# A hybrid decoder layer: both feed-forward products by seven products of quarters, with sums added in DRAM

## The chip, the core and the metric

The kernel runs on one core of a Trainium2 chip. The time is the device time of one execution, in microseconds; the lower it is, the better. TensorE (PE) has a clock that the chip grants at one of two levels, 1.2 and 2.4 GHz; the profile shows 2.4 GHz as a granted clock of 1.00 and 1.2 GHz as 0.50.

## The reference

One layer on a sequence of 512 tokens, 2048 wide, with 8192 hidden columns, all in float32:

```
h = rms_norm(x)
p = h @ w_in                      # three kinds of heads: gating MLP, short conv, dilated attention
x = x + concat(A, B, C) @ w_out
h = rms_norm(x, mlp_norm)
x = x + square(relu(h @ w_mlp_in)) @ w_mlp_out
```

The change concerns the last two lines: a product of 512 x 2048 by 2048 x 8192, which the text calls the first product (FF1), and one of 512 x 8192 by 8192 x 2048, the second product (FF2).

## The kernel before

**Three matmuls for a product.** Every float32 operand is split into a high part and a low part. ScalarE (ACT) rounds to the high part (a cast), VectorE (DVE) subtracts it to get the low part, and a product is then high by high, high by low, and low by high, summed in PSUM (`mm3`, L162 to L164). Activations lie transposed, with features on the 128 partitions and the 512 tokens along the free dimension. A weight tile is the stationary operand and a matmul is 512 or 256 tokens wide. `wh` and `wl` are the parts of weights, three buffers each; `xhl` holds the parts of the normalised activations (later of hidden tiles), `pt` is a PSUM tile.

**Plain groups.** A group of 512 output columns (`tr_group`) has eight pieces of weights, of two K-tiles (128 rows of the contraction) each: the piece is loaded (`wr`, in the pool's tag "raw", three buffers), cast, its low part subtracted, and then multiplied, 4 column tiles x 3 matmuls for each K-tile. Weights are prepared two pieces ahead (AHEAD = 2, `stream`).

**Groups of seven products.** Twenty-nine groups of FF1, of 256 columns each, are done with the scheme of Strassen and Winograd: the operands are cut into quarters, seven products of quarters take the place of eight, and each one needs sums of quarters. The class `Strassen` loads four quarters of the weights (`wq`, L821), forms sums of them (`ws` and in place, L826 to L832), splits each of the seven operands, multiplies (`product`, L845 and L846), and combines the results in an output tile `c` (six parts of 256 columns) with `p` as room for products 0 and 3 (L849, L862). A step of a product is a pair of matmuls: one of 512 (high weights by high and low activations side by side) and one of 256 (low weights by high activations), and DVE adds the two halves afterwards. The activations' sums (`tt`, four operands with high and low parts) are made once, by tasks, in FF1's first plain group (`x_sums`, L784, from the float32 activations `xg` in the pool "x1"). That pool is closed before the first quarter is loaded, and the pool "quarters" is opened in its place. `c` has a single buffer there. It is stored to `hd` in DRAM (L877).

**Order.** `tasks` is a list of small pieces of work: after each K-tile of a plain group, and after each product of a seven-product group, `step` runs the next one, so that this work stands between weights on DVE and ACT; `flush` runs all that are left. In FF1 a scheduler sets the order. From FF1's last group on, DVE and ACT work in the order of the program (`ordr`); matmuls and DMAs are still ordered by the scheduler. A hidden tile is read back from `hd` by GpSimd's (POOL's) queue (L899), squared with relu, multiplied by the reciprocal mean square `rbc` (L903, L904) and split, by `hid_tasks`.

**FF1 and FF2.** FF1 is one plain group of 512 columns, 29 seven-product groups, one plain group of 256. FF2 goes through the hidden columns in four chunks of 2048, and in each through four plain groups of 512 output columns. The sums over chunks stay in SBUF: `acc`, 16 tiles, starts as the residual `x1d` (L939) and each group's PSUM is added to it (L950). Two buffers (`hid` and `xhl`) hold the hidden tiles of alternate chunks. The last group's last pieces are ordered by output tile, with the final tile in two halves of 256.

## Time and profile before

| | before |
|---|---|
| time, median of three runs | 2067.32 us (2066.99 to 2067.97) |
| time of the profiled execution | 2066.59 us |
| its span in the profile | 2064.9 us |
| TensorE busy | 2051.5 us, 99% |
| VectorE busy | 1198.2 us, 58% |
| ScalarE busy | 677.5 us, 33% |
| GpSimd busy | 100.6 us, 5% |
| mean granted clock | 0.999 |

The span is the time between the first and the last instruction that the profiler recorded on the core; the rest of the execution's time lies around it. Busy shares are means over the whole span. The rest of the profile is read by stages: the time of each engine in a stretch, the price of one instruction of a given shape, and, at a hole in an engine's work, what ended it (written behind the instruction as the idle time and its releaser). Matmuls overlap, so the price of one is the distance between starts, not its own duration; the same is true of DVE to a small degree.

### The profile page before, as it was taken

The numbers are of one execution on the slowest core, as the hardware profiler recorded it, in microseconds if no ns is written. First come the engines' busy times: TensorE is split into PE (matmuls) and PEld (weight loads), VectorE is DVE, ScalarE is ACT, GpSimd is POOL, SyncE is SP. The second block draws the span as 40 slices with busy tenths as digits, with TensorE's granted clock in tenths as the row PEclk, the third lists the DMA queues.
The fourth block names the chain that finished last, engine by engine and source line by source line (L and its number), as shares of the span: only waits on it lengthen the run. The fifth ranks groups of instructions, "written<-read, shape, count | busy, mean of one in ns | idle before, by whom it ended". The sixth has DMA issues, their size and how long they took to land.

```text
span 2064.9 us, 25736 instructions
## 1 busy us (share of the span) xinstructions
PE 2051.5 (99%) x10274; PEld 1751.2 (85%) x10274; DVE 1198.2 (58%) x1675; ACT 677.5 (33%) x905; POOL 100.6 (5%) x194
## 2 busy tenths in 40 slices
PE   9999999999999999999999999989999999999999
PEld 9999888888888888888888888878888888888888
DVE  5443453534334489899998998866624632652222
ACT  5334442322233443344334333333312321322121
POOL 0000000100000000000000000120100000000000
PEclk9999999999999999999999999999999999999999
DMA  7423222433533454444444344364433432432332
GB/s 248 133 75 108 72 72 69 125 99 97 193 113 123 130 148 141 145 122 141 132 126 148 121 141 128 103 241 156 143 101 108 147 114 100 136 124 95 119 116 82
DMA packets 247016, 259.69 MB, mean 126 GB/s; under 512 B 11748, under 2 KB 179940, under 8 KB 246896
## 3 DMA queue, kind: packets, MB, share of 16 engines
q1 hardware_dynamic: 229888, 206.08, 32.3%
q0 software_dynamic: 14560, 47.75, 6.7%
q10 hardware_dynamic: 2448, 4.23, 0.6%
q8 instruction: 80, 1.31, 0.3%
q14 instruction: 40, 0.33, 0.1%
HBM read 232.81 MB, written 25.19 MB: 125 GB/s over the span
## 4 chain that ended last, share of the span: by engine, by line
PE 71%; issue 26%; POOL 2%; DMA 0%; DVE 0%; ACT 0%; POOLq 0%; DVEq 0%; ACTq 0%
PE pt L162 18%; PE pt L163 18%; PE pt L164 18%; PE pn L162 5%; PE pn L163 5%; PE pn L164 5%; POOL hd L877 1%; PE pt L845 1%; PE pt L846 1%; PE sc L529 0%; PE et L542 0%; PE qt L463 0%; ACT wh L262 0%; DMA acc<-x1d 0%; PE warm L124 0%
## 5 line engine op out<-in xcount | busy, mean ns | idle before, releaser
L263 DVE TENSOR_TENSOR wl<-wr,wh 128x1024 fp32r<-128x1024 f32 (+2 forms) x287 | 321.4, 1121 | 612.3 <-ACT wh L262 574.8
L262 ACT CAST wh<-wr 128x1024 fp32r<-128x1024 f32 (+2 forms) x287 | 277.5, 968 | 710.7 <-PE pt L163 578.7
L162 PE MATMUL pt<-xhl,wh 128*128 128x512 f32 (+1 forms) x912 | 352.6, 387 | 0.0
L163 PE MATMUL pt<-xhl,wh 128*128 128x512 f32 (+1 forms) x912 | 351.6, 386 | 0.0
L164 PE MATMUL pt<-xhl,wl 128*128 128x512 f32 (+1 forms) x912 | 351.5, 385 | 0.0
L845 PE MATMUL pt<-tt,wh 128*128 128x512 f32 x928 | 330.5, 399 | 0.0
L846 PE MATMUL pt<-tt,wl 128*128 128x256 f32 x928 | 260.6, 281 | 0.0
L845 PE MATMUL pt<-xhl,wh 128*128 128x512 f32 x696 | 248.5, 399 | 0.0
L262 ACT CAST wh<-wq 128x1024 fp32r<-128x1024 f32 x145 | 152.3, 1050 | 246.2 <-PE pt L845 233.8
L845 PEld LDWEIGHTS pt<-tt,wh 128*128 128x128 f32 x928 | 174.4, 188 | 43.6
L162 PE MATMUL pt<-hid,wh 128*128 128x512 f32 x512 | 200.4, 391 | 6.9 <-ACT wh L262 6.9
L263 DVE TENSOR_TENSOR wl<-wq,wh 128x1024 fp32r<-128x1024 f32 x145 | 177.1, 1222 | 43.5 <-ACT wh L262 40.9
L162 PEld LDWEIGHTS pt<-xhl,wh 128*128 128x128 f32 x912 | 171.3, 188 | 34.6 <-issue 0.2
L164 PEld LDWEIGHTS pt<-xhl,wl 128*128 128x128 f32 x912 | 171.3, 188 | 34.6
L163 PEld LDWEIGHTS pt<-xhl,wh 128*128 128x128 f32 x912 | 171.3, 188 | 34.2 <-issue 0.2
L163 PE MATMUL pt<-hid,wh 128*128 128x512 f32 x512 | 199.9, 391 | 0.0
L164 PE MATMUL pt<-hid,wl 128*128 128x512 f32 x512 | 198.2, 390 | 0.1
L846 PE MATMUL pt<-xhl,wl 128*128 128x256 f32 x696 | 195.5, 281 | 0.0
L162 PE MATMUL pn<-wh,xhl 128*128 128x384 f32 (+2 forms) x512 | 185.8, 366 | 1.3 <-DVE qn L440 1.3
L163 PE MATMUL pn<-wl,xhl 128*128 128x384 f32 (+2 forms) x512 | 179.4, 350 | 0.0
L164 PE MATMUL pn<-wh,xhl 128*128 128x384 f32 (+2 forms) x512 | 179.3, 350 | 0.0
L846 PEld LDWEIGHTS pt<-tt,wl 128*128 128x128 f32 x928 | 175.3, 189 | 0.0
(203 smaller groups left out, 2571.9 us busy)
## 6 DMA issues: line engine op xcount, KB each, us to landing
wr<-in_w_mlp_out_dram SPq DMA_DIRECT2D x128, 512.0 KB, 3.5
wq<-in_w_mlp_in_dram SPq DMA_DIRECT2D x116, 512.0 KB, 4.1
wr<-in_w_in_dram SPq DMA_DIRECT2D x144, 128.0 KB, 2.4
wr<-in_w_out_dram SPq DMA_DIRECT2D x32, 512.0 KB, 3.5
hd<-c POOLq DMA_DIRECT2D x58, 256.0 KB, 2.6
hs<-hd POOLq DMA_DIRECT2D x56, 256.0 KB, 2.9
wr<-in_w_in_dram SPq DMA_DIRECT2D x24, 512.0 KB, 3.5
wr<-in_w_in_dram SPq DMA_DIRECT2D x31, 384.0 KB, 3.5
```

Source lines behind the costliest of these rows:

```text
L162: nc.tensor.matmul(ps, lhsT=ah, rhs=bh, start=start, stop=False)
L163: nc.tensor.matmul(ps, lhsT=ah, rhs=bl, start=False, stop=False)
L164: last[0] = nc.tensor.matmul(ps, lhsT=al, rhs=bh, start=False, stop=stop)
L262: ordr(nc.scalar.copy(out=dst_h, in_=src))
L263: ordr(nc.vector.tensor_tensor(out=dst_l, in0=src, in1=dst_h.bitcast(F32), op=ALU.subtract))
L845: nc.tensor.matmul(pv, lhsT=h[:, m], rhs=b, start=m == 0, stop=False)
L846: nc.tensor.matmul(pv[:, 1], lhsT=l[:, m], rhs=b[:, 0], start=False, stop=m == KT // 2 - 1)
L877: nc.gpsimd.dma_start(out=hd[self.c0 // P + n], in_=c[:, 2 + 2 * n:4 + 2 * n].rearrange("p h t -> p (h t)"))
```

## The change

- **FF1.** The first plain group has 256 columns in place of 512, and there are 30 seven-product groups. In these, products 0, 1 and 3 stay as pairs of 512 and 256 columns; products 2, 4, 5 and 6 become three matmuls of 256 (`mm3`), which leave one half of PSUM each, and product 6 uses the other half of product 5's bank.
- **Hidden values.** relu, the factor 1/rms and the square are computed before the store to `hd` (`hidden`: one DVE step and one ACT Square), so that `rbc` now holds 1/rms from a reciprocal root (`stat_x1`) and `hd` holds finished hidden values.
- **FF2.** In each chunk the groups are seven-product groups of 256 columns, six in the last three chunks and four in chunk 0, and plain groups of 512: one at the end of each chunk and one more at the start of chunk 0. A seven-product group has products 2 and 3 as pairs.
- **Parts of hidden tiles.** `xh` and `xl` (the two halves of `xhl`) hold the parts of one chunk, and `tt` its four sums. Those of the next chunk are written over them while the chunk's last plain group runs (`both_tasks`: 18 tasks, pairs of hidden tiles read in advance into three buffers). Chunk 0's are made by `parts_tasks` during FF1's last group and FF2's first.
- **Sums over chunks.** `acc` is gone. In chunks 0 to 2 a group's result goes through `c` and is added to `x1d` in DRAM by an accumulating DMA (`accum_op`). In the last chunk `x1d` is loaded, added on DVE and stored as the output. `c_tiles` hands a plain group's four results through the same single `c`, two to a tile.
- **Buffers.** Quarters of `wq` have three buffers in place of five, and those with k = 1 are in "raw" now. DVE's sums in `Strassen` are in program order from FF1's last group on.

```diff
-        nc.vector.reciprocal(out=rbc, in_=ssum)
+        rsqrt(rbc, ssum, *[mlp["x1"].tile([P, T], F32, tag="sq", name=f"rsb_{n}", bufs=2) for n in "sy"])
...
                 for f, k in ((0, 0), (1, 0), (1, 1), (0, 1)):
-                    if (f, k) == (1, 1):
+                    if k:
                         t = wpool.tile([P, KT // 2, P], F32, tag="raw", name=f"wq{i}{f}{k}")
                     else:
-                        t = sp.tile([P, KT // 2, P], F32, tag="wq", name=f"wq{i}{f}{k}", bufs=5)
-                    nc.sync.dma_start(out=t, in_=w1[:, k::2, self.c0 + f * P:self.c0 + (f + 1) * P])
+                        t = sp.tile([P, KT // 2, P], F32, tag="wq", name=f"wq{i}{f}{k}", bufs=3)
+                    nc.sync.dma_start(out=t, in_=self.src[:, k::2, self.c0 + f * P:self.c0 + (f + 1) * P])
...
         def product(self, j, h, l):
             sp, i = mlp["spool"], self.i
-            pv = main_ps(f"pt{j}{i}").rearrange("p (h t) -> p h t", h=2)
+            if j == 0 and self.begin is not None:
+                self.begin(self)
+            if j == 2:
+                flush()
+            if j < 6:
+                self.pv = main_ps(f"pt{j}{i}").rearrange("p (h t) -> p h t", h=2)
+            pv, half, double = self.pv, int(j == 6), j in self.double
...
+                start, stop = m == 0, m == KT // 2 - 1
+                bh, bl, both = self.factor(FACTOR[j], m)
+                if double:
+                    nc.tensor.matmul(pv, lhsT=h[:, m], rhs=both, start=start, stop=False)
+                    last[0] = nc.tensor.matmul(pv[:, 1], lhsT=l[:, m], rhs=bh, start=False, stop=stop)
+                else:
+                    mm3(pv[:, half], (h[:, m], l[:, m]), (bh, bl), start, stop)
 
             def take(out, more):
-                add(out, pv[:, 0], more)
-                add(out, pv[:, 1], out)
+                add(out, pv[:, half], more)
+                if double:
+                    add(out, pv[:, 1], out)
...
-            elif j == 5:
-                take(c[:, 3], c[:, 0])
             elif j == 6:
-                take(c[:, 4], c[:, 1])
-            if j == 6:
-                for n in range(2):
-                    nc.gpsimd.dma_start(out=hd[self.c0 // P + n], in_=c[:, 2 + 2 * n:4 + 2 * n].rearrange("p h t -> p (h t)"))
...
+                add(c[:, 3:5], pv, c[:, 0:2])
+                self.finish(self, c[:, 2:6].rearrange("p (f h) t -> p f (h t)", f=2))
...
+    def open_quarters():
+        flush()
+        close_right("x1")
+        mlp["spool"] = open_right("quarters")
+
+    def hidden(c, src, rb):
+
+        ordr(nc.vector.scalar_tensor_tensor(out=c, in0=src, scalar=0.0, in1=rb, op0=ALU.max, op1=ALU.mult))
+        ordr(nc.scalar.activation(out=c, in_=c, func=AF.Square))
+
+    def finish_in(g, c):
+        hidden(c, c, rbc.unsqueeze(1).broadcast_to([P, 2, T]))
+        for n in range(2):
+            nc.gpsimd.dma_start(out=hd[g.c0 // P + n], in_=c[:, n])
...
-        def rest(n):
-            t, k = room.pop(n), ks[n]
-            ordr(nc.vector.scalar_tensor_tensor(out=t, in0=t, scalar=0.0, in1=t, op0=ALU.max, op1=ALU.mult))
-            ordr(nc.vector.tensor_tensor(out=t, in0=t, in1=rbc, op=ALU.mult))
-            split(d[:, 0, k], d[:, 1, k], t)
-            load(n + ahead)
...
+                cc = mlp["spool"].tile([P, 6, TH], F32, tag="c", name=f"{name}{j}").rearrange("p (f h) t -> p f (h t)", h=2)
+            yield j, ps, cc[:, j % 2]
...
+    def close_mlp_in(pss, f0):
+        for j, ps, c in c_tiles(pss, f"cn{f0}"):
+            hidden(c, ps, rbc)
+            nc.gpsimd.dma_start(out=hd[f0 + j], in_=c)
...
+    def sums(t):
+        q = t.rearrange("p k (h t) -> p (k h) t", h=2)
+        sub(q[:, 0], q[:, 1], q[:, 0])
+        sub(q[:, 1], q[:, 3], q[:, 1])
+        sub(q[:, 3], q[:, 3], q[:, 0])
+        sub(q[:, 2], q[:, 2], q[:, 3])
+        return q
...
+    def parts_tasks(c):
+
+        room = [load_pair(c, m) for m in range(3)]
+        s = [slice(2 * m, 2 * m + 2) for m in range(8)]
+
+        def parts(m):
+            if m < 8:
+                high(xh[:, s[m]], room[m])
+            if m:
+                low(xl[:, s[m - 1]], room[m - 1], xh[:, s[m - 1]])
+                room.append(load_pair(c, (m + 2) % 8) if m < 9 else None)
+
+        def rest(m):
+            t = room[8 + m]
+            q = sums(t)
+            high(mlp["tt"][:, :, m, 0], q)
+            return q
+
+        kept = {}
+
+        def even(m):
+            kept[m] = rest(m)
+
+        def odd(m):
+            low(mlp["tt"][:, :, m, 1], kept[m], mlp["tt"][:, :, m, 0])
+            if m + 3 < 8:
+                room.append(load_pair(c, m + 3))
+
+        out = [lambda m=m: parts(m) for m in range(9)]
+        for m in range(8):
+            out.extend([lambda m=m: even(m), lambda m=m: odd(m)])
+        return out
+
+    def both_tasks(c):
+
+        room = {m: load_pair(c, m) for m in range(3)}
+        kept = {}
+
+        def tile_high(k):
+            if k < KC:
+                high(xh[:, k], room[k // 2][:, k % 2])
+
+        def tile_low(k):
+            if 0 <= k < KC:
+                low(xl[:, k], room[k // 2][:, k % 2], xh[:, k])
+
+        def even(m):
+            tile_high(2 * m)
+            tile_low(2 * m - 1)
+            if m:
+                kept[m - 1] = sums(room[m - 1])
+                high(mlp["tt"][:, :, m - 1, 0], kept[m - 1])
+
+        def odd(m):
+            tile_high(2 * m + 1)
+            tile_low(2 * m)
+            if m:
+                low(mlp["tt"][:, :, m - 1, 1], kept[m - 1], mlp["tt"][:, :, m - 1, 0])
+                if m + 2 < KC // 2:
+                    room[m + 2] = load_pair(c, m + 2)
+
+        return [f for m in range(KC // 2 + 1) for f in (lambda m=m: even(m), lambda m=m: odd(m))]
...
-    def close_mlp_out(pss, ng):
-        for j in range(4):
-            dst = mlp["acc"][:, 4 * ng + j]
-            ordr(nc.vector.tensor_tensor(out=dst, in0=pss[j], in1=dst, op=ALU.add))
...
+        tasks.extend([None] * 9 + parts_tasks(0))
...
+    def finish_out(g, c):
+        for n in range(2):
+            nc.gpsimd.dma_start(out=x1d[g.c0 // P + n], in_=c[:, n], accum_op=ALU.add)
+
+    def load_sum(f0):
+        t = pair("acc")
+        for n in range(2):
+            nc.gpsimd.dma_start(out=t[:, n], in_=x1d[f0 + n])
+        return t
+
+    def begin_last(g):
+        g.acc = load_sum(g.c0 // P)
+
+    def finish_last(g, c):
+        add(g.acc, c, g.acc)
+        for n in range(2):
+            nc.gpsimd.dma_start(out=out_v[:, g.c0 // P + n], in_=g.acc[:, n])
+
+    def open_mlp_out(c, f0):
+        if c == nch - 1:
+            mlp["acc"] = [load_sum(f0), load_sum(f0 + 2)]
+        elif f0:
+            tasks.extend(both_tasks(c + 1))
+
+    def close_mlp_out(pss, c, f0):
+        for j, ps, t in c_tiles(pss, f"co{c}{f0}"):
+            ordr(nc.scalar.copy(out=t, in_=ps))
+            nc.gpsimd.dma_start(out=x1d[f0 + j], in_=t, accum_op=ALU.add)
...
-    nch = DFF // CHUNK_FF
-    groups.append(tr_group(w1[:, :, :T], 4, x1mov, lambda pss: close_mlp_in(pss, 0)))
-    for c0 in range(T, DFF - 2 * P, 2 * P):
-        groups.append(Strassen(c0))
+    groups.append(tr_group(w1[:, :, :2 * P], 2, x1mov, lambda pss: close_mlp_in(pss, 0)))
+    for c0 in range(2 * P, DFF - 2 * P, 2 * P):
+        groups.append(Strassen(w1, c0, x1_factor, (0, 1, 3), finish_in))
     groups.append(tr_group(
-        w1[:, :, DFF - 2 * P:], 2, x1mov, lambda pss: close_last_in(pss, DFF // P - 2), before=open_last_in,
+        w1[:, :, DFF - 2 * P:], 2, x1mov, lambda pss: close_mlp_in(pss, DFF // P - 2), before=open_last_in,
     ))
     for c in range(nch):
-        for ng in range(4):
-            tail = c == nch - 1 and ng == 3
-            close = close_last if tail else close_last_group if c == nch - 1 else close_mlp_out
+        src = w2[:, c * KC:(c + 1) * KC]
+        tail = c == nch - 1
+
+        for f0 in ([0] if c == 0 else []) + [KT - 4]:
+            if f0:
+                for c0 in range(0 if c else T, f0 * P, 2 * P):
+                    groups.append(Strassen(
+                        src, c0, hid_factor, (2, 3), finish_last if tail else finish_out, begin_last if tail else None,
+                    ))
             groups.append(tr_group(
-                w2[:, c * KC:(c + 1) * KC, ng * T:(ng + 1) * T], 4, hmov(c),
-                (lambda ps, j, ts: close_last(ps, 3, j, ts)) if tail else lambda pss, ng=ng, close=close: close(pss, ng),
-                before=lambda c=c, ng=ng: open_mlp_out(c, ng), tail=tail,
+                src[:, :, f0 * P:f0 * P + T], 4, hmov,
+                (lambda ps, j, ts, f0=f0: close_last(ps, f0, j, ts)) if tail else lambda pss, c=c, f0=f0: close_mlp_out(pss, c, f0),
+                before=lambda c=c, f0=f0: open_mlp_out(c, f0), tail=tail,
             ))
```

On DVE in one of FF2's plain groups, before, from the middle of the group (`hs` is a hidden tile read back, `wl` the low part of a weight piece):

```order
L263 TENSOR_TENSOR wl_12373<-wr_12371,wh_12372 128x1024
L903 SCALAR_TENSOR_TENSOR hs_12301<-hs_12301 128x512
L904 TENSOR_TENSOR hs_12301<-hs_12301,rbc 128x512
L263 TENSOR_TENSOR xhl<-hs_12301,xhl 128x512
L950 TENSOR_TENSOR acc<-pt_0_12121,acc 128x512
L950 TENSOR_TENSOR acc<-pt_1_12122,acc 128x512
L950 TENSOR_TENSOR acc<-pt_2_12123,acc 128x512
L950 TENSOR_TENSOR acc<-pt_3_12124,acc 128x512
L263 TENSOR_TENSOR wl_12411<-wr_12409,wh_12410 128x1024
L263 TENSOR_TENSOR wl_12449<-wr_12447,wh_12448 128x1024
```

And after, in the last plain group of chunk 0 (`hr` is a pair of hidden tiles; the four subtractions in place are the sums):

```order
L262 TENSOR_TENSOR wl_13732<-wr_13730,wh_13731 128x1024
L784 TENSOR_TENSOR xhl<-hr_13614,xhl 128x512
L784 TENSOR_TENSOR hr_13614<-hr_13614 128x256 x4
L784 TENSOR_TENSOR xhl<-hr_13684,xhl 128x512
L784 TENSOR_TENSOR tt<-hr_13614,tt 128x4x256
L262 TENSOR_TENSOR wl_13775<-wr_13773,wh_13774 128x1024
L784 TENSOR_TENSOR xhl<-hr_13684,xhl 128x512
L784 TENSOR_TENSOR hr_13684<-hr_13684 128x256 x4
L784 TENSOR_TENSOR xhl<-hr_13727,xhl 128x512
L784 TENSOR_TENSOR tt<-hr_13684,tt 128x4x256
L262 TENSOR_TENSOR wl_13818<-wr_13816,wh_13817 128x1024
```

Between two weight pieces there now stand two low parts of tiles, four sums and the low parts of the sums; the additions into `acc` are gone.

On ACT in the same place of the kernel before, casts of tiles and of weight pieces take turns:

```order
L262 CAST xhl<-hs_11893 128x512
L262 CAST wh_12004<-wr_12003 128x1024
L262 CAST xhl<-hs_11929 128x512
L262 CAST wh_12040<-wr_12039 128x1024
L262 CAST xhl<-hs_11965 128x512
L262 CAST wh_12076<-wr_12075 128x1024
```

After, the same plain group's end and the start of the next chunk's first seven-product group (`wq` and `ws` are its operands of products 0, 1, 2 and so on; `co` are the plain group's results on the way to the accumulating DMA):

```order
L943 CAST xhl<-hr_13813 128x512
L943 CAST tt<-hr_13770 128x4x256
L943 CAST xhl<-hr_13813 128x512
L261 CAST wh_13909<-wq_13865 128x1024
L943 CAST xhl<-hr_13856 128x512
L943 CAST tt<-hr_13813 128x4x256
L943 CAST xhl<-hr_13856 128x512
L1042 COPY co_13947<-pt_0_13604 128x512
L1042 COPY co_13947<-pt_1_13605 128x512
L1042 COPY co_13952<-pt_2_13606 128x512
L1042 COPY co_13952<-pt_3_13607 128x512
L261 CAST wh_13958<-ws_13868 128x1024
```

The four copies of `co` have moved in front of the cast of product 2's weights, behind casts of sums (`tt`) that were not there before.

On DVE at FF1's entrance, before (`xg` are the float32 sums in the making, the last `wl<-wq` belongs to the first seven-product group):

```order
L315 RECIPROCAL rbc<-ssum 128x512
L263 TENSOR_TENSOR wl_5865<-wr_5863,wh_5864 128x1024
L784 TENSOR_TENSOR xg<-xg 128x4x256 x2
L263 TENSOR_TENSOR tt<-xg,tt 128x4x256
L263 TENSOR_TENSOR wl_5901<-wr_5899,wh_5900 128x1024
L263 TENSOR_TENSOR tt<-xg,tt 128x4x256
L784 TENSOR_TENSOR xg<-xg 128x4x256
L263 TENSOR_TENSOR wl_5937<-wr_5935,wh_5936 128x1024
L263 TENSOR_TENSOR tt<-xg,tt 128x4x256
L263 TENSOR_TENSOR wl_5990<-wq_5978,wh_5989 128x1024
L826 TENSOR_TENSOR ws_5986<-wq_5980,wq_5982 128x1024
```

And after, in the same place:

```order
L262 TENSOR_TENSOR tt<-xg,tt 128x4x256
L277 SCALAR_TENSOR_TENSOR rbc<-rsb_s,rsb_y 128x512
L262 TENSOR_TENSOR tt<-xg,tt 128x4x256
L262 TENSOR_TENSOR wl_5881<-wr_5879,wh_5880 128x2x256
L784 TENSOR_TENSOR xg<-xg 128x4x256 x2
L262 TENSOR_TENSOR tt<-xg,tt 128x4x256
L784 TENSOR_TENSOR xg<-xg 128x4x256
L262 TENSOR_TENSOR tt<-xg,tt 128x4x256 x2
L905 SCALAR_TENSOR_TENSOR cn_5954<-pt_0_5764,rbc 128x512
L905 SCALAR_TENSOR_TENSOR cn_5954<-pt_1_5765,rbc 128x512
L262 TENSOR_TENSOR wl_5922<-wq_5910,wh_5921 128x1024
```

The reciprocal has become a root with steps around it, the weight pieces are of half width, and relu with the factor of the plain group's results (`cn`) stands between the last sum and the first quarter's low part.

## Rows read from the trace of the kernel before

**Rows 1.** The page, section 1: busy us, share of the span, instructions.

```profile
PE 2051.5 (99%) x10274; PEld 1751.2 (85%) x10274; DVE 1198.2 (58%) x1675; ACT 677.5 (33%) x905; POOL 100.6 (5%) x194
```

**Rows 2.** Windows: first, 29, last groups of FF1; FF2: PE, PEld, DVE, ACT, POOL.

```profile
714.90:759.02 44.12, 44.12 (x195) 36.18 (x194) 36.15 (x35) 22.59 (x29) 2.04 (x4) 1.00 0.55 153
759.02:1332.90 573.88, 573.88 (x3250) 497.65 (x3249) 516.51 (x692) 228.74 (x264) 34.56 (x64) 1.00 0.44 131
1332.90:1354.50 21.60, 21.60 (x97) 17.84 (x95) 16.92 (x27) 7.57 (x13) 2.16 (x4) 1.00 0.52 172
1354.50:2061.20 706.70, 699.65 (x3120) 579.46 (x3118) 312.14 (x366) 170.01 (x187) 39.58 (x74) 1.00 0.38 126
```

**Rows 3.** Timeline of PE, FF2, 512 columns: start, duration; 20 starts.

```profile
1799.64 0.39 PE L164 MATMUL pt<-hid,wl 128*128 128x512 f32 x1
...
1803.95 0.39 PE L162 MATMUL pt<-hid,wh 128*128 128x512 f32 x1
```

**Rows 4.** Timeline of PE, end of FF2, 256 columns; 24 starts.

```profile
2058.31 0.28 PE L162 MATMUL pt<-xhl,wh 128*128 128x256 f32 x1
...
2061.06 0.28 PE L164 MATMUL pt<-xhl,wl 128*128 128x256 f32 x1
```

**Rows 5.** Timeline of PE near the start of FF2.

```profile
1370.78 0.39 PE L164 MATMUL pt<-hid,wl 128*128 128x512 f32 x1
1375.81 0.79 PE L162 MATMUL pt<-hid,wh 128*128 128x512 f32 x1 [4.64 <-ACT wh L262]
```

**Rows 6.** Windows, 3 us behind that wait.

```profile
1375.80:1378.80 3.00, 2.99 (x7) 2.41 (x8) 2.51 (x3) 0.42 (x1) 1.68 (x4) 0.50 0.50 160
```

**Rows 7.** Timeline of DVE at the entrance of the seven-product groups.

```profile
718.20 0.68 DVE L757 TENSOR_TENSOR xg<-pt,xg 128x512 f32<-128x512 f32 x1
...
743.46 1.23 DVE L263 TENSOR_TENSOR wl<-wr,wh 128x1024 fp32r<-128x1024 f32 x1 [1.24 <-ACT wh L262]
744.60 1.22 DVE L263 TENSOR_TENSOR tt<-xg,tt 128x1024 fp32r<-128x1024 f32 x1
752.46 1.23 DVE L263 TENSOR_TENSOR wl<-wq,wh 128x1024 fp32r<-128x1024 f32 x1 [6.63 <-ACT wh L262]
753.60 1.22 DVE L826 TENSOR_TENSOR ws<-wq,wq 128x1024 f32<-128x1024 f32 x1
754.85 1.22 DVE L828 TENSOR_TENSOR ws<-ws,wq 128x1024 f32<-128x1024 f32 x1
```

**Rows 8.** Timeline of ACT, same place.

```profile
751.38 1.05 ACT L262 CAST wh<-wq 128x1024 fp32r<-128x1024 f32 x1 [7.00 <-DMA wq<-in_w_mlp_in_dram]
...
756.84 1.27 ACT L885 COPY cn<-pt 128x512 f32<-128x512 f32 x2
...
763.50 1.07 ACT L885 COPY cn<-pt 128x512 f32<-128x512 f32 x2 [3.80 <-DMA hd<-cn]
```

**Rows 9.** Groups by form, seven-product groups of FF1: busy, mean ns, idle before.

```profile
L263 DVE TENSOR_TENSOR wl<-wq,wh 128x1024 fp32r<-128x1024 f32 x124 | 151.5, 1222 | 32.5 <-ACT wh L262 30.2
...
L262 ACT CAST wh<-wq 128x1024 fp32r<-128x1024 f32 x124 | 130.2, 1050 | 206.8 <-PE pt L845 204.7 <-PE pt L846 2.1
...
L849 DVE TENSOR_TENSOR c<-pt,c 128x256 f32<-128x256 f32 x197 | 83.0, 421 | 10.4 <-PE pt L846 6.2
...
L877 POOL DMA_DIRECT2D hd<-c x49 | 26.5, 540 | 452.8 <-DVE c L849 452.8
```

**Rows 10.** Tile wq in these groups: issue to landing.

```profile
DMA to landing us min/median/max: 3.8/4.1/4.7
```

**Rows 11.** Tile hd in these groups, stores.

```profile
DMA to landing us min/median/max: 2.3/2.7/4.0
```

**Rows 12.** Tile acc at the start of FF2, loads of x1d.

```profile
DMA to landing us min/median/max: 3.0/5.4/6.5
```

**Rows 13.** Groups of instructions by form, FF2.

```profile
L263 DVE TENSOR_TENSOR xhl<-hs,xhl 128x512 fp32r<-128x512 f32 x32 | 22.2, 692 | 22.0 <-ACT xhl L262 22.0
L262 ACT CAST xhl<-hs 128x512 fp32r<-128x512 f32 x32 | 19.9, 622 | 85.5 <-DVE hs L904 85.5
```

More of the change, by code (lines that the diff above doesn't have):

```diff
@@ L797, in trunk_kernel, with __init__ @@
     class Strassen:
-        FACTOR = [0, 1, 5, 3, 4, 2, 6]
-        def __init__(self, c0):
-            self.c0, self.pieces, self.open_, self.before_load = c0, range(7), None, None
-            self.banks = []
+        def __init__(self, src, c0, factor, double, finish, begin=None):
+            self.src, self.c0, self.factor, self.double = src, c0, factor, double
+            self.finish, self.begin = finish, begin
+            self.pieces, self.open_, self.before_load = range(7), None, None
         def load(self, j):
@@ L861, in product @@
                 p = self.p[j // 3]
-                nc.scalar.copy(out=p, in_=pv[:, 0])
-                add(p, pv[:, 1], p)
+                ordr(nc.scalar.copy(out=p, in_=pv[:, 0]))
+                if double:
+                    add(p, pv[:, 1], p)
             elif j == 1:
@@ L881, in close_mlp_in, with c_tiles @@
+    def c_tiles(pss, name):
         for j, ps in enumerate(pss):
             if j % 2 == 0:
[L883 to L910 removed]
+                cc = mlp["spool"].tile([P, 6, TH], F32, tag="c", name=f"{name}{j}").rearrange("p (f h) t -> p f (h t)", h=2)
+            yield j, ps, cc[:, j % 2]
@@ new lines, in high, with low @@
+    def high(dst, src):
+        ordr(nc.scalar.copy(out=dst, in_=src))
+    def low(dst, src, h):
+        sub(dst, src, h.bitcast(F32))
+    def parts_tasks(c):
[23 more added lines that the diff above has]
+        return out
@@ L961, in trunk_kernel, with hmov @@
+    def hmov(k):
+        return xh[:, k], xl[:, k]
     groups = [
```

117 lines of the change are left out of this document (40 added, 77 removed).

## The prediction

> **What bounds the kernel now.** First the page's busy shares [rows 1]: TensorE (PE) works 2051.5 of 2064.9 us, so time is lost or won by what it streams and where it stands still. Second the stretches [rows 2]: in the 29 seven-product groups of the first product (FF1) it is busy every microsecond, 573.88 / 29 = 19.79 us a group; VectorE (DVE) works 516.51 of these 573.88 us, 17.8 a group, so it is close behind. In the second product (FF2) it is busy 699.65 of 706.70. Third, in the timeline, the price of one matmul: 512 columns start (1803.95 - 1799.64) / 19 = 0.2267 us apart [rows 3], 256 columns (2061.06 - 2058.31) / 23 = 0.1196 [rows 4]; a pair of 512 and 256 is 19.79 / 56 = 0.3534 [rows 2]. Fourth, the one large hole: after 1370.78 TensorE waits 4.64 us for a weight cast [rows 5] and comes back at half clock, 0.50 or 1.2 GHz [rows 6]. Against 16 x 192 x 0.2267 = 696.4 us of streaming FF2 loses 706.7 - 697.0 = 9.7 us, all near its start (0.6 us of fill is in the 697.0).
>
> **(a) FF2's streaming.** 256 columns cost 96 x 0.2267 = 21.76 us in plain form. A seven-product group costs 16 pairs x 0.3534 + 40 x 3 x 0.1196 = 20.0. 22 groups: 22 x 1.76 = -38.5.
>
> **(b) FF1's streaming.** 256 plain columns become a group: 19.96 - 21.76 = -1.8. All other groups now cost 24 x 0.3534 + 32 x 3 x 0.1196 = 19.96, as four products take three matmuls of 256 for a pair: 29 x 0.17 = +4.9. Together +3.1.
>
> A rule speaks for more here: the Trainium skill (TensorE: Matmul & The Clock Gate, section Wait — 56ns, not 53.3ns?) has matmuls start N / 2.4 GHz + about 2.5 ns apart, 109 ns at 256 columns. This trace has 119.6, so the measurement decides; by the page a group would be near 18.3 and a plain 256 near 20.7, an estimate that would add some 14 us to the gain of (a).
>
> **(c) The hole at FF2's start.** The hidden tiles are now made ahead, while FF1's last group and FF2's first plain group run: the tasks do 16 tiles' parts beside plain pieces of 5.44 us (24 x 0.2267). I take the whole loss away: -9.7; what is late next is (f).
>
> **(d) FF1's entrance.** DVE's sums for the seven products begin after 718.20, and the last one's low part ends at 744.60 + 1.22 = 745.82 [rows 7]. The pool that holds them is closed then and the quarters of weights go into its room, so their DMAs wait for it: cast at 751.38 after 7.00 us of idleness ended by the DMA [rows 8], 5.55 us after the sums. Before, the plain group of 44.12 us [rows 2] covered that up to 759. Now it takes 22.2 and ends near 737. DVE's 27.6 us shrink by six weight lows of half width (1.22 - 0.69, 3.2 us) and the idle 1.24 at 743.46 [rows 7, 13], and grow by three steps of 512 for the reciprocal root (2.1): sums end near 743.5, quarters land at 749.05, cast 1.05 [rows 9], first product 750.1. TensorE waits 13 and another 1.2 for the low part: +14.5. The ends are 12.4 and 18.4: no row shows the new Sqrt, 0 to 2.5 us, and the other quarters may be later.
>
> **(e) FF1's steady groups.** DVE gets relu and the factor 1/rms for 1024 columns (1.22, as a low part [rows 9]) and loses some adds, since four products have one half to take. About 18 us of 19.96, so DVE is no bound by itself, but there is a loop through buffers: three for the k = 1 quarters and plain weights, and one for the output tile c. Low part of product 6 frees a quarter; load 4.1 [rows 10], cast 1.05, low 1.14 (start to start, 753.60 - 752.46 [rows 7]), sum 1.14, take of product 6 0.69, low of product 2 1.14, relu 1.22, Square 1.05, store 0.54 + 2.7 [rows 9, 11], three adds into the freed c 3 x 0.42 [rows 9], then low 5, sum, low 6 at 1.14 each, 3.4: 19.5, and 0.3 for handoffs, 19.8 against 19.96. It just fits; by the longest landings, 4.7 and 4.0 [rows 10, 11], it is 21.7. I take +3 (a tenth of a microsecond a group), ends 0 and +20 (nearly half of the way to the longest, which come seldom).
>
> **(f) Boundaries plain to seven products in FF2.** There are four. Take those from one chunk to the next (three). While the plain group runs, the tasks make the next chunk's parts. Per piece the order makes one loop of two engines: ScalarE (ACT) cast of weights 1.05, DVE low 1.14, tile low 0.69, four sums of 256 at 0.42, then ACT's high of the sums 1.05 and tile high 0.62 [rows 9, 13]: 6.2 against TensorE's 5.44, 0.7 late a piece, and near 1.6 in the last two, where two weight sums (1.14) stand as well. Over seven pieces that is 5 x 0.7 + 2 x 1.6, ACT 6.7 late. Weights of products 0 and 1 stand ahead of that, those of product 2 don't: on ACT, ahead of their cast, are the four copies of the plain group's results, two of them into the single tile c, which must be stored before the third. Before, this took 763.50 - 756.84 = 6.66 us from first copy to third, ended by the store [rows 8]. So product 2's weights come 6.7 + 6.7 + 1.2 + 1.05 = 15.7 us after the plain group, wanted at 5.7 (two products): 10. Smaller waits for low parts and the last tiles, 0.3 to 1.7 each, add about 4: 14 each, 42 for three. At the first boundary the tasks are not as late (by about 4): 10. Sum +52.
>
> The store is now an accumulating one, of which the trace has none. Bounds: as a plain store, 2.3 at the shortest [rows 11], which takes 1.4 off a boundary and with half the lateness makes (f) 38; as a store behind a load of the same tile, 2.7 + 5.4 [rows 11, 12], 4 to 5 more a boundary and a second one behind it, 75. I take the plain one, which is the nearest row in kind. The Trainium skill (Collectives: The Full Stack, section The bandwidth ceiling: the fold count and why AG ≠ RS ≠ AR) says that an add inside a transfer needs two source reads and so moves at half the rate; no run here shows it yet. By it a store would be an estimated 5.4 for 2.7 and (f) some 11 us more.
>
> **(g) The clock.** After a wait of 4.64 the clock was at 0.50 for 3.0 us [rows 5, 6], a loss of 1.5. Six waits of that length, partly counted: +3, ends 0 and +6.
>
> **Sum.** From this execution's span: 2064.9 - 38.5 + 3.1 - 9.7 + 14.5 + 3 + 52 + 3 = 2092.3. Around the span lie 2066.59 - 2064.9 = 1.69: **2094 us**. That execution is 0.73 under the median of 2067.32, so 2095 against the median: 1.3% slower. Own range of this case: lows 2064.9 - 45.1 + 12.4 + 0 + 38 + 0 + 1.7 = 2072; highs 2064.9 - 45.1 + 18.4 + 20 + 75 + 6 + 1.7 = 2141.
>
> **Rivals.** *The streams decide* (faster). TensorE's program takes rows of products 0 to 4 in mixed order at the boundaries, and the two pieces of lookahead could swallow the late casts. It decides if ACT begins the copies no later than the plain group's end and c's stores land in the shortest time. Without (e) to (g): 2064.9 - 45.1 + 14.5 + 1.7 = 2036; with (f) halved, 2062. Against it: single c and the copies' place on ACT, which no lookahead passes. *FF1's loop is too long and accumulating stores double* (much slower). Every microsecond over 19.96 costs 30. For it: the margin is 0.2 us, and landings spread by 0.9 and 1.7 [rows 10, 11]; against: DVE's order may let takes go earlier. At 21.4 it is +43: 2135, with stores doubled 2146. *It does not get its groups*: rest of the kernel unchanged, seven products lose in waits exactly what they gain, 2067; I see no reason for it but chance.
>
> **How the numbers follow.** Forecast 0.66, faster rival 0.14, much slower rival 0.17, balance 0.03. The range takes 2062 (the faster rival with half of its waits) to 2132 (most of the own range and the mild part of the slower rival), leaving some 0.1 at either end. 0.2%, 4 us, is what a measurement tells from no change: faster 0.14, within 0.04, slower 0.82, as nearly all of the own range lies above 2071.
>
> **What would show it.** FF1's first plain group near 22 us, then 13 us of idle TensorE ended by a cast or low of wq; groups of 20.0; no wait of 4 us near FF2's start; four holes of 6 to 11 us in FF2, at product 2, ended by ACT's cast of ws, and in front of that cast copies of co, the third waiting for a store. Wrong if these holes are ended by something else or are under 4 us, or if FF1's groups take over 20.3.

## The result and the profile after

The changed kernel takes 2113.49 us (median of four runs, 2111.53 to 2115.12) against 2067.44 of the kernel before: a ratio of 1.0222, with a 95% interval of 1.0205 to 1.024. The forecast was 2095, in a range of 2062 to 2132, slower with a chance of 0.82. The profiled execution has a span of 2112.1 us.

The page's busy shares, first section, and below them the windows of four stages, cut nearly as in [rows 2]: FF1's first plain group; its 30 seven-product groups; its last plain group together with FF2's first, which [rows 2] has in its fourth window; the rest of FF2. The columns are the same: PE, PEld, DVE, ACT, POOL, granted clock, DMA share, GB/s. Beside the last three kernels of the table of experiments, four of 19 runs of the kernel before took 2056 to 2058 us for a reason that the record does not show, which widens the intervals there and raises those ratios against those of the medians.

```profile
PE 2035.8 (96%) x12482; PEld 1837.7 (87%) x12482; DVE 1407.9 (67%) x1864; ACT 825.1 (39%) x1094; POOL 158.0 (7%) x270
```

```profile
714.90:749.95 35.05, 23.34 (x101) 18.23 (x99) 30.44 (x36) 21.36 (x31) 2.69 (x5) 0.90 0.45 133
749.95:1351.62 601.67, 601.52 (x4320) 567.48 (x4321) 521.17 (x600) 263.95 (x300) 34.32 (x64) 1.00 0.45 134
1351.62:1417.91 66.29, 65.76 (x290) 53.83 (x289) 42.48 (x54) 27.91 (x31) 16.01 (x30) 1.00 0.66 218
1417.91:2109.10 691.19, 633.73 (x4161) 579.02 (x4159) 499.62 (x620) 264.28 (x320) 83.34 (x124) 0.96 0.52 136
```

TensorE's busy time fell from 2051.5 [rows 1] to 2035.8 us, so the products did become cheaper, and yet the span grew by 47 us. The lost time stands in two places: 35.05 us for a plain group of 256 columns at FF1's entrance, of which TensorE worked 23.34, and FF2 from 1417.91 on, 691.19 us of which it worked 633.73, at a mean clock of 0.96.

**The entrance.** Rows of the timelines of DVE, ACT and TensorE, in that order, each in a fence of its own (start, duration, engine and line, operation, and in brackets the idle time before with its releaser; the last four rows of TensorE belong to the boundaries further down):

```profile
741.64 2.42 DVE L262 TENSOR_TENSOR tt<-xg,tt 128x1024 fp32r<-128x1024 f32 x2
```

```profile
748.85 1.99 ACT L261 CAST wh<-wq 128x1024 fp32r<-128x1024 f32 x2 [2.75 <-DMA wq<-in_w_mlp_in_dram]
```

```profile
749.95 0.80 PE L867 MATMUL pt<-xhl,wh 128*128 128x512 f32 x1 [10.72 <-ACT wh L261]
...
1437.43 0.79 PE L867 MATMUL pt<-tt,wh 128*128 128x512 f32 x1 [10.57 <-ACT wh L261]
...
1578.76 0.79 PE L867 MATMUL pt<-tt,wh 128*128 128x512 f32 x1 [11.26 <-ACT wh L261]
...
1762.64 0.80 PE L867 MATMUL pt<-tt,wh 128*128 128x512 f32 x1 [11.07 <-ACT wh L261]
...
1945.47 0.80 PE L867 MATMUL pt<-tt,wh 128*128 128x512 f32 x1 [10.49 <-ACT wh L261]
```

The last sum ends at 741.64 + 2.42 = 744.06, the first quarter's cast starts at 748.85, the first product at 749.95: the chain of [rows 7, 8], earlier by some two microseconds, with a plain group in front of it that ends twenty microseconds sooner (at 749.95 - 10.72 = 739.23, against 759.02 in [rows 2]).

Behind that wait TensorE starts at half clock. The windows of the first seven-product group and of the other 29 (PE, PEld, DVE, ACT, POOL, clock, DMA):

```profile
749.95:772.00 22.05, 21.90 (x145) 20.11 (x146) 21.56 (x24) 8.69 (x10) 1.08 (x2) 0.92 0.53 163
772.00:1351.62 579.62, 579.62 (x4178) 547.36 (x4177) 499.61 (x577) 255.26 (x290) 33.24 (x62) 1.00 0.45 133
```

The first takes 22.05 us, each of the others 579.62 / 29 = 19.99, and in these TensorE is busy without a gap.

**The boundaries.** The other four rows of that fence are all of TensorE's waits above 2.1 us in FF2. Each stands before the first matmul of product 2, where a seven-product group follows a plain one. What ACT did before the second of them (its timeline, the end of chunk 0):

```profile
1558.57 1.05 ACT L943 CAST tt<-hr 128x1024 fp32r<-128x1024 f32 x1 [3.89 <-DVE hr L784]
...
1565.50 1.05 ACT L943 CAST tt<-hr 128x1024 fp32r<-128x1024 f32 x1 [3.89 <-DVE hr L784]
...
1566.97 1.06 ACT L1042 COPY co<-pt 128x512 f32<-128x512 f32 x2
1576.69 1.07 ACT L1042 COPY co<-pt 128x512 f32<-128x512 f32 x2 [8.66 <-DMA x1d<-co]
1577.65 1.06 ACT L261 CAST wh<-ws 128x1024 fp32r<-128x1024 f32 x1
```

The plain group's last matmul is followed by product 0 at 1559.82. ACT begins the copies of its results at 1566.97, 7.15 us later, held up by a loop in which it waits 3.89 us for DVE's sums and which takes 1565.50 - 1558.57 = 6.93 us for the last piece. Then come 1576.69 - 1566.97 = 9.72 us from the first copy to the third (8.75 to 9.72 at the four boundaries), against 6.66 in [rows 8], and only then the cast for product 2.

**The other groups of FF2.** Two group starts in TensorE's timeline, and DVE's timeline inside the group after them:

```profile
1617.67 0.28 PE L161 MATMUL pt<-xhl,wh 128*128 128x256 f32 x1
...
1638.54 0.28 PE L161 MATMUL pt<-xhl,wh 128*128 128x256 f32 x1
```

```profile
1628.43 0.42 DVE L787 TENSOR_TENSOR c<-pt,p 128x256 f32<-128x256 f32 x1 [4.09 <-DMA x1d<-c]
```

This group took 20.87 us. In the last chunk, where `c` is added on DVE and stays in SBUF, groups take 20.05, so this is no matter of the matmuls. DVE waited 4.09 us in program order for the accumulating store of the group before to let go of the single `c`, and low parts of weights were queued behind that add.

### The profile page after: what moved, and what is told of

The parts are those of the page before. It is cut to its first block, busy times and chain, and to the rows that moved or that the text cites. A ratio compares the mean times of both kernels' runs of the same rounds, so it can differ in the third digit from the quotient of the medians.

```text
span 2112.1 us, 30790 instructions
## 1 busy us (share of the span) xinstructions
PE 2035.8 (96%) x12482; PEld 1837.7 (87%) x12482; DVE 1407.9 (67%) x1864; ACT 825.1 (39%) x1094; POOL 158.0 (7%) x270
## 4 chain that ended last, share of the span: by engine, by line
PE 73%; DMA 10%; DVE 9%; ACT 4%; issue 3%; POOL 0%; SPq 0%; ACTq 0%; DVEq 0%
PE pt L161 14%; PE pt L163 14%; PE pt L162 14%; PE pt L867 10%; PE pt L868 5%; PE pn L161 5%; PE pn L163 5%; PE pn L162 5%; DMA x1d<-c 4%; DVE wl L262 3%; DMA wq<-in_w_mlp_out_dram 3%; DVE hr L784 2%; ACT wh L261 2%; DMA x1d<-co 1%; DVE c L787 1%
## 5 line engine op out<-in xcount | busy, mean ns | idle before, releaser
L163 PE MATMUL pt<-xhl,wl 128*128 128x256 f32 (+1 forms) x1456 | 482.5, 332 | 4.6 <-DVE wl L262 4.6
L161 PE MATMUL pt<-xhl,wh 128*128 128x256 f32 (+1 forms) x1456 | 482.5, 332 | 1.9 <-ACT xhl L943 1.5
L162 PE MATMUL pt<-xhl,wh 128*128 128x256 f32 (+1 forms) x1456 | 483.0, 332 | 1.1 <-DVE xhl L784 1.1
L262 DVE TENSOR_TENSOR wl<-wr,wh 128x1024 fp32r<-128x1024 f32 (+2 forms) x199 | 209.5, 1053 | 346.9 <-ACT wh L261 301.4
L261 ACT CAST wh<-wq 128x1024 fp32r<-128x1024 f32 x260 | 272.8, 1050 | 385.3 <-PE pt L162 196.2
L262 DVE TENSOR_TENSOR wl<-wq,wh 128x1024 fp32r<-128x1024 f32 x260 | 317.4, 1221 | 81.4 <-ACT wh L261 79.6
L161 PE MATMUL pt<-tt,wh 128*128 128x256 f32 x1072 | 303.7, 283 | 1.1 <-ACT wh L261 1.0
L163 PEld LDWEIGHTS pt<-xhl,wl 128*128 128x128 f32 x1456 | 276.3, 190 | 32.4 <-DVE wl L262 6.5
L162 PE MATMUL pt<-tt,wh 128*128 128x256 f32 x1072 | 303.5, 283 | 0.0
L161 PEld LDWEIGHTS pt<-xhl,wh 128*128 128x128 f32 x1456 | 275.9, 190 | 28.4 <-ACT xhl L943 2.1
L162 PEld LDWEIGHTS pt<-xhl,wh 128*128 128x128 f32 x1456 | 276.4, 190 | 27.7 <-DVE xhl L784 1.7
L867 PE MATMUL pt<-tt,wh 128*128 128x512 f32 x592 | 218.6, 409 | 43.8 <-ACT wh L261 43.7
L161 PEld LDWEIGHTS pt<-tt,wh 128*128 128x128 f32 x1072 | 204.2, 191 | 5.9 <-ACT wh L261 2.4
L162 PEld LDWEIGHTS pt<-tt,wh 128*128 128x128 f32 x1072 | 204.3, 191 | 0.0
L867 PEld LDWEIGHTS pt<-tt,wh 128*128 128x128 f32 x592 | 114.7, 194 | 70.0 <-ACT wh L261 45.2
```

The costliest lines, as they stand in the source:

```text
L161: nc.tensor.matmul(ps, lhsT=ah, rhs=bh, start=start, stop=False)
L162: nc.tensor.matmul(ps, lhsT=ah, rhs=bl, start=False, stop=False)
L163: last[0] = nc.tensor.matmul(ps, lhsT=al, rhs=bh, start=False, stop=stop)
L261: ordr(nc.scalar.copy(out=dst_h, in_=src))
L262: ordr(nc.vector.tensor_tensor(out=dst_l, in0=src, in1=dst_h.bitcast(F32), op=ALU.subtract))
L867: nc.tensor.matmul(pv, lhsT=h[:, m], rhs=both, start=start, stop=False)
```

## The experiments

Times are medians. The table is worked out from the starts of groups in TensorE's timelines: the length of the seven-product group behind a plain one (in the order of the four boundaries), and by how much all other seven-product groups of FF2 together exceed 20.05 us.

| kernel | time, us | groups behind a plain one | others' excess |
|---|---|---|---|
| changed kernel | 2113.5 | 37.20, 37.21, 37.02, 36.46 | 6.7 |
| plain stores of co | 2096.9 | 32.76, 32.11, 32.44, 32.14 | 6.4 |
| plain stores of c | 2106.3 | 37.06, 37.04, 37.29, 36.18 | 0 |
| both stores plain | 2089.9 | 32.11, 32.08, 32.10, 32.18 | 0 |
| co in pair tiles | 2097.7 | 29.14, 28.44, 28.44, 28.45 | 23.2 |
| co in pair tiles, next pairs loaded late | 2103.1 | 29.40, 33.86, 33.79, 33.78 | 10.4 |
| all results in pair tiles | 2073.2 | 28.00, 28.45, 28.46, 28.67 | 1.0 |
| the same, sums' high parts later | 2062.2 | 27.50, 23.76, 25.21, 27.43 | 0 |
| the same, FF1's first group wide | 2047.8 | 27.15, 25.18, 23.67, 28.06 | 0 |

**What the accumulating store costs.** Three runs take the accumulation away; the first only from the plain groups' results, the second only from those of seven-product groups:

```diff
-            nc.gpsimd.dma_start(out=x1d[f0 + j], in_=t, accum_op=ALU.add)
+            nc.gpsimd.dma_start(out=x1d[f0 + j], in_=t)
```

> The changed kernel with the stores of the plain groups' results (co) as plain stores: the sums of those columns over the chunks are left out, nothing else. Theory A (the accumulating store holds the single tile c): from the first to the third copy 9.7 us become about 6.7, as in the kernel before, at each of four boundaries: -12 us, 2101. Rival B (the copies are late because the loop of tasks is, and what the store does is hidden): the hole at product 2 stays at 10.5 to 11.3 us and the time within 3 us of 2113. Rival C (the store lands late because hidden tiles and quarters are loaded beside it): 9.7 stays 9 or more.

Measured: 2096.94 us, 1.0146 of the kernel before (1.0129 to 1.0163). ACT's timeline at the same boundary:

```profile
1562.50 1.06 ACT L1042 COPY co<-pt 128x512 f32<-128x512 f32 x2
1567.13 1.07 ACT L1042 COPY co<-pt 128x512 f32<-128x512 f32 x2 [3.57 <-DMA x1d<-co]
```

From first to third copy it is 4.63 us in place of 9.72. So theory A holds and the price is larger than it said: 5.1 us a turn here, and 16.5 us in all, where 12 were expected. Rival B falls, as the wait shrinks with the store, and so does rival C, which had the turn stay at 9 us or more.

```diff
-            nc.gpsimd.dma_start(out=x1d[g.c0 // P + n], in_=c[:, n], accum_op=ALU.add)
+            nc.gpsimd.dma_start(out=x1d[g.c0 // P + n], in_=c[:, n])
```

> The changed kernel with the stores of the seven-product groups' results in chunks 0 to 2 as plain stores: the sums over chunks of those columns are left out. Theory A (a group of FF2 takes 20.7 us in place of 20.06 because DVE's first add into c waits for the accumulating store of the group before): groups of chunks 0 to 2 fall to 20.1, 16 x 0.65 = -10 us, 2103. Rival B (the quarters' loads or DVE's own order set the pace): groups stay near 20.7, 2113.

Measured: 2106.34 us, 1.0191 (1.0176 to 1.0206): -7.2. Every group of FF2 that is not behind a plain one takes 20.05. The tile `c` in FF2's chunks 0 to 2, from issue to landing, in the changed kernel and then in this one:

```profile
DMA to landing us min/median/max: 3.6/6.8/8.4
```

```profile
DMA to landing us min/median/max: 2.4/3.1/4.7
```

The same bytes go from the same tile to the same place, 6.8 us with the sum and 3.1 without. The quarters' loads are not what sets those groups' pace (rival B falls). The expected 10 us had taken all 16 groups to be 0.65 us too long; it was 6.7 us, in 13 groups.

> The changed kernel with all its accumulating stores as plain stores: no column's sum over the chunks is made in chunks 0 to 2. If the two effects of accumulating are apart (the boundary's by co, the other groups' by c): -16.5 - 7.2 = -23.7, 2090; boundary groups 32 to 33 us and all others 20.05. If they share the DMA engines' time: less than 20 together, or more than 27.

Measured: 2089.92 us, 1.0112 (1.0095 to 1.0128): -23.6, the sum of the two. The effects are apart. What is left at a boundary without any accumulation is 32.1 - 20.05 = 12 us, which leaves the loop of tasks and the turn through the single tile; the next runs take these away.

**Who holds whom at a boundary.** The plain groups' results go through two tiles of the hidden pairs' buffers:

```diff
-        for j, ps, t in c_tiles(pss, f"co{c}{f0}"):
-            ordr(nc.scalar.copy(out=t, in_=ps))
-            nc.gpsimd.dma_start(out=x1d[f0 + j], in_=t, accum_op=ALU.add)
+        for j, ps in enumerate(pss):
+            if j % 2 == 0:
+                cc = pair("co")
+            ordr(nc.scalar.copy(out=cc[:, j % 2], in_=ps))
+            nc.gpsimd.dma_start(out=x1d[f0 + j], in_=cc[:, j % 2], accum_op=ALU.add)
```

> The changed kernel, in which the plain groups' four results are copied to two tiles of the hidden pairs' buffers (free there) in place of the single c; stores stay accumulating. Theory A (copies behind the single tile make the holes): the third copy follows the second at once, 8.7 us less before product 2's cast, the hole at product 2 falls from 11 to about 2.5 us and the clock stays at 1.00: -8.6 x 4 and some 1.5 x 4 of half clock, 2073. Rival B (the loop of tasks makes them): -2 us a boundary, 2105.

Measured: 2097.70 us, 1.0146 (1.013 to 1.0161). ACT's timeline at the boundary and in the group behind it:

```profile
1563.49 2.04 ACT L1044 COPY co<-pt 128x512 f32<-128x512 f32 x4
...
1587.25 1.05 ACT L261 CAST wh<-wq 128x1024 fp32r<-128x1024 f32 x1 [7.09 <-DMA wq<-in_w_mlp_out_dram]
```

Half of this came as expected: the four copies follow each other, the hole before product 2 shrinks from 11.26 to 2.50 us, and the boundary's group from 37.2 to 28.4, 33 us over the four. But 16.5 of these are given back: in the next group ACT waits 7.09 us for a quarter to land, the four such groups take 23.5 to 26.4 us, and the others are no shorter. The forecast of 2073 for this run missed that.

A run that moved the first loads of the next chunk's hidden pairs away from there, by letting them wait for the matmul issued last before the plain group:

```diff
+            ins = nc.gpsimd.dma_start(out=t[:, n], in_=hd[c * KC + 2 * m + n])
+            if late:
+                behind(ins)
...
-        room = {m: load_pair(c, m) for m in range(3)}
+        room = {m: load_pair(c, m, True) for m in range(3)}
```

> The run with co in pairs, and the first three pairs of hidden tiles of each next chunk (1.5 MB) are loaded only when the chunk's last plain group begins, in place of right behind the boundary before. Theory A (these loads stood beside the quarters of the group behind a boundary, whose last quarter landed 7 us late there): the groups behind the boundaries between chunks fall from 23.5 to 26.4 us to under 21.5, while the plain group may start its tasks 3 us later: 2097.7 - 9 = 2089. Rival B (accumulating stores alone make the quarter late): these groups stay at 23 to 26 us, 2097 or a little more.

Measured: 2103.05 us, 1.0174 (1.0158 to 1.0189), a step back as a whole, where 2089 was expected, and yet an answer. The second groups behind the four boundaries fall from 24.78, 23.90, 26.42 and 23.48 us to 20.95, 20.05, 22.45 and 23.06. At the first three, from which the loads were taken away, 11.7 of 15.0 us of excess are gone, though the third stays over the 21.5 that was expected; at the fourth, where no such loads stand, little changes. So most of the excess at the first three came with the pair loads beside the quarters, and rival B falls there. But tasks that start later are later at the end (ACT begins the copies at the end of chunk 0 12.5 us behind the plain group, against 7.14 in the run before), so the boundaries between chunks grow from 28.4 to 33.8. Here the loads of hidden pairs have to be early and apart from the quarters, not late.

**More tiles instead of one.** All results are put together in pair tiles, four buffers in place of three, and `c` keeps two inner parts, so that the room in SBUF stays the same. The four buffers of pairs are then in use by results until a chunk's last groups, so the loads of the next chunk's hidden pairs can't begin at the boundary:

```diff
-                self.c = sp.tile([P, 6, TH], F32, tag="c", name=f"c{i}")
+                self.c = sp.tile([P, 2, TH], F32, tag="c", name=f"c{i}")
+                self.o = pair("o")
...
-                add(c[:, 3:5], pv, c[:, 0:2])
-                self.finish(self, c[:, 2:6].rearrange("p (f h) t -> p f (h t)", f=2))
+                add(o[:, 1:3], pv, c)
+                self.finish(self, self.o)
...
-                cc = mlp["spool"].tile([P, 6, TH], F32, tag="c", name=f"{name}{j}").rearrange("p (f h) t -> p f (h t)", h=2)
+                cc = pair(name)
```

> The changed kernel, in which all results on their way to DRAM (of seven-product groups and of plain groups) are put together in tiles of the hidden pairs' kind, four buffers in place of three, and c keeps only its two inner parts. Theory A (accumulating stores that land in 5 to 8 us hold the single c): boundary groups as in the run with co in pairs, 28.4 us in place of 37, and the other groups of chunks 0 to 2 at 20.05 as in the run with plain stores; the group behind a boundary no longer takes 24, since no hidden tiles are loaded just there: -35 -7 +0, 2072. Rival B (the DMA traffic itself makes the quarters late, whoever holds the tile): the group behind a boundary stays at 24 and others at 20.7 to 20.9: 2097 as with co alone.

Measured: 2073.15 us, 1.0041 (1.0025 to 1.0057). The accumulating stores out of these tiles land no faster:

```profile
DMA to landing us min/median/max: 3.9/6.9/8.5
```

That is the tile `o` in chunks 0 to 2, 6.9 us as before, and DVE and ACT wait 0.4 us for these stores in all, against 49.5 us that DVE waits for the stores of `c` in the changed kernel: groups take 20.05 and the ones behind a boundary 28.5. GpSimd's timeline in the chunk after the second boundary has the loads of hidden pairs near its end; in the kernel with co in pairs they stood right behind the boundary:

```profile
1658.75 1.73 POOL L1020 DMA_DIRECT2D x1d<-o  x2 [18.32 <-DVE o L787]
1659.84 2.85 POOL L933 DMA_DIRECT2D hr<-hd  x4
1668.28 1.07 POOL L933 DMA_DIRECT2D hr<-hd  x2 [5.59 <-DMA x1d<-o]
```

So the accumulating stores cost time through the buffer that they held, not by their own traffic, and rival B falls in what it expected. The traffic of the pair loads is not cleared by this: they have moved away from the quarters in this run, and the run before showed what they cost beside them.

**The loop of tasks.** In the same kernel the sums' high parts are cast, and their low parts made, one pair of tiles later, so that ACT does not wait for sums that DVE is just making. A pair is held longer by that, and four pairs are loaded in advance in place of three:

```diff
-        room = {m: load_pair(c, m) for m in range(3)}
+        room = {m: load_pair(c, m) for m in range(4)}
...
-            if m:
+            if m > 1:
+                high(mlp["tt"][:, :, m - 2, 0], kept[m - 2])
+            if 0 < m < 9:
                 kept[m - 1] = sums(room[m - 1])
-                high(mlp["tt"][:, :, m - 1, 0], kept[m - 1])
...
-            if m:
-                low(mlp["tt"][:, :, m - 1, 1], kept[m - 1], mlp["tt"][:, :, m - 1, 0])
+            if m > 1:
+                low(mlp["tt"][:, :, m - 2, 1], kept[m - 2], mlp["tt"][:, :, m - 2, 0])
```

> The same, and in the tasks the high parts of the sums come one pair of tiles later, so that ACT does not wait 3.9 us for DVE's sums in every piece of a plain group. Theory A (prediction's step f: the tasks' loop of 6.9 us a piece against 5.44 makes ACT some 7 us late at a boundary): the copies of co begin within 2 us of the plain group's end at the three boundaries between chunks, 3 to 5 us less each: -12 against the run before, 2060. Rival B (what is late behind the copies is DVE's and stays): within 3 us of the run before.

Measured: 2062.20 us, 11 less than the run before, as theory A has it; 0.9994 of the kernel before (0.9975 to 1.0014), which is no difference that can be told. ACT's timeline at the end of chunk 0, where product 0 starts at 1548.62:

```profile
1546.62 1.05 ACT L945 CAST tt<-hr 128x1024 fp32r<-128x1024 f32 x1
...
1549.34 1.07 ACT L1045 COPY co<-pt 128x512 f32<-128x512 f32 x2
```

The cast of the sums waits for nothing now, and the copies begin 0.7 us behind the plain group in place of 7.15, as they do at the two later boundaries between chunks. The fourth pair is not what did it: in neither of the two runs does ACT or DVE wait for the landing of a hidden pair in these plain groups. The three groups behind become 4.7, 3.2 and 1.2 us shorter, the last of them less than the 3 to 5 that were expected.

**The entrance by itself.** The changed kernel with FF1's first group as it was:

```diff
-    groups.append(tr_group(w1[:, :, :2 * P], 2, x1mov, lambda pss: close_mlp_in(pss, 0)))
-    for c0 in range(2 * P, DFF - 2 * P, 2 * P):
+    groups.append(tr_group(w1[:, :, :T], 4, x1mov, lambda pss: close_mlp_in(pss, 0)))
+    for c0 in range(T, DFF - 2 * P, 2 * P):
```

> The changed kernel with FF1's first plain group 512 columns wide again and 29 seven-product groups. Theory A (the entrance waits for the sums and the quarters' loads whatever TensorE has to do): the first seven-product group starts at 759 in place of 751, but one group of 20.06 us less: -12 us, 2101, and no wait over 1 us at the entrance. Rival B (the wait of 10.7 us is of the narrow group's own making, by its order on DVE): the entrance waits as before or the time moves under 4 us.

Measured: 2100.90 us, 1.0162 (1.0147 to 1.0178): -12.6. TensorE's timeline at the entrance has no wait left:

```profile
758.74 0.39 PE L163 MATMUL pt<-xhl,wl 128*128 128x512 f32 x1
758.97 0.39 PE L867 MATMUL pt<-xhl,wh 128*128 128x512 f32 x1
```

**All together.** The wide first group, all results in pair tiles, the sums' high parts later:

> The same, with FF1's first plain group 512 wide. If the entrance's cost is independent of what FF2 does: another -12.5 us, 2048, under the kernel before (2067). If the gains of the boundaries are given back by late quarters: 2065 to 2085.

Measured: 2047.78 us (2047.38 to 2048.83), 0.9926 of the kernel before (0.9899 to 0.9952), faster than both kernels; its slowest run lies under the kernel before's fastest (2056.05). The page's first section of this kernel:

```profile
PE 2025.3 (99%) x12434; PEld 1832.4 (90%) x12434; DVE 1404.2 (69%) x1897; ACT 822.4 (40%) x1086; POOL 157.8 (8%) x270
```

TensorE is at 99% again, as in [rows 1], with 26 us less to do.

## Why the prediction was right, and by how much it was off

| step | predicted, us | in the profile after, us |
|---|---|---|
| (a) FF2's streaming | -38.5 | 22 x (20.05 - 21.77) = -37.8 |
| (b), (e) FF1's groups | +3.1 and +3 | 601.67 - 573.88 - 21.77 = +6.0, of it 2.1 half clock behind the entrance |
| (c) hole at FF2's start | -9.7 | 66.29 - (21.60 + 53.2) = -8.5 |
| (d) entrance | +14.5 | 35.05 - 21.77 = +13.3, the half clock behind it stands in (b) |
| (f), (g) boundaries and clock | +52 and +3 | 147.89 - 4 x 20.05 = +67.7 |
| other groups of FF2 | none | +6.7 |
| sum | +27.4 | +47.4, measured 2112.1 - 2064.9 = 47.2 |

**(a) to (d) held, (e) by luck.** The matmul prices of [rows 2 to 4] give the groups to 0.05 us (22 x 1.76 is 38.7, not 38.5; that changes nothing). The entrance was forecast step by step: sums end at 743.5 (744.06), first product at 750.1 (749.95). In between, the plain group ended at 739.23 and not near 737, so the wait was 10.7 us in place of 13, with the same first product. Undoing the narrow group gives back 12.6 us; from the stages it is 13.3 + 2.1 of half clock - 1.8, which 256 more plain columns cost, or 13.6. The much slower rival, which FF1 groups of over 20.3 us would have shown, did not come. But step (e)'s +3, a tenth of a microsecond a group for waits in the loop through the buffers, did not come either: 29 groups take 19.99 us without a gap. FF1's total fits because the first group's 2.1 us at half clock, for which (g) had a term of its own, and 0.03 us a group in the price of matmuls took that place.

**(f) named the right mechanism and mis-sized one term.** The loop of tasks was put at 6.2 us a piece and 7.0 in the last two, and ACT at 6.7 us late; the last one takes 6.93, and ACT is 7.15 late. The copies through the single tile were put at 6.7 us, the price of a plain store's turn [rows 8], as "the nearest row in kind". That choice is the step that failed: the turn takes 9.72 at the end of chunk 0. There the first matmul of product 2 starts 1578.76 - 1559.82 = 18.94 us behind the plain group, where 15.7 was forecast, and 3.0 of these 3.2 us are the turn. Over the four boundaries the turns are 10.2 us longer than forecast. The row was also too dear for what it stood for: with plain stores the turn at this place takes 4.63 us, so the accumulating store adds 5.1 to it, and it was luck that the row covered 2.0 of them. The upper end, a landing of 2.7 + 5.4 = 8.1 us, was nearer: the results of seven-product groups land in 6.8, those of the plain groups in 3.7 to 8.2.

The Trainium skill (Collectives: The Full Stack, section The bandwidth ceiling: the fold count and why AG ≠ RS ≠ AR) says of the reducing step of collectives in a ring that its add needs two source reads, which halves the rate. The prediction took this over to a store, which is no such step, and the size agrees: 6.8 us to landing against 3.1 for `c`, and a turn of 9.72 against 4.63 for `co`, though the median landing of `co` is 4.7 against 3.5. That two reads are the cause is not shown by any run.

The first boundary, inside chunk 0, was put at 10 us, since the tasks there were taken to be less late. ACT began its copies 1426.61 - 1417.91 = 8.70 us behind the plain group there, and the group lost as much as the others (37.20).

**One effect was not in the sum.** The longer store holds `c` past the next group's first add, 6.7 us over 13 groups. Step (e) had weighed just this loop for FF1, where the store is plain, and did not ask it again for FF2, where it is not. The run with plain stores of `c` takes it to nothing. The forecast's direction and mechanism did not hang on it.

**The faster rival** (streams decide) needed ACT on time and the shortest stores, and neither was the case. The last run comes nearer to it: with the tile, the loop and the entrance mended, FF2's shorter streams show.

**Open.** In the best run the four groups behind plain ones still take 23.7 to 28.1 us. At the first boundary ACT's copies still begin 1410.04 - 1403.61 = 6.43 us late, as chunk 0's `parts_tasks` kept their order, and product 2 waits 2.79 us for its cast; at the last one DVE waits 3.30 us for an accumulating store of `co` to let go of a pair tile, and product 2 then 2.83 us for DVE, so a held buffer is left even there. What each of the smaller waits, and the clock after them, costs was not taken apart. Why the quarters of the group behind the fourth boundary were late with `co` in pairs stays open as well.

## What to carry to other kernels

Before a result goes to an accumulating store out of a single buffer, price the turn of that buffer with the store's longer landing, not with a plain store's, and ask at every place in the loop who writes the buffer next. Where two engines make something in turns, read one round of the ping-pong off the order and set it against TensorE's time for the piece; one step of delay between producer and consumer, at the price of a fourth pair loaded in advance, brought 11 us here. Work that makes the matmuls cheaper shortens also the cover that hid loads and sums, so the same edit wants the cover counted again.
